# Side pairs of a modulation dealt out anew over two stages of a hybrid diffusion block

## The chip, the cores and the metric

The kernel runs on one core of one Trainium2 chip. The metric is the device time of one execution in microseconds (us), compared as the median of a few timed executions. Beside the timed executions there is one profiled execution, whose rows tell when each instruction ran on the engines: PE (TensorE, matmuls; PEld is its loading of the stationary operand), DVE (VectorE), ACT (ScalarE), POOL (GpSimd) and SP (SyncE, which here only issues transfers).

## The reference, cut to what matters

One layer over 256 latent tokens and 256 context tokens of width 2048, all in 32-bit floats. A vector `c` gives six modulation vectors of 2048 numbers each (`mod`); three of them (`sh1`, `sc1`, `g1`) serve the mixing half, three (`sh2`, `sc2`, `g2`) the MLP half.

```python
mod = (s_lat @ ada_w[l] + ada_b[l])[:, None, :]          # s_lat = silu(c), ada_w: 2048 x 12288
sh1, sc1, g1, sh2, sc2, g2 = jnp.split(mod, N_MOD, axis=-1)
h = modulate(rmsnorm(x, norm1_g[l]), sh1, sc1)
hc = modulate(rmsnorm(xc, norm1_g[l]), csh1, csc1)
q, k, v, f, hy = split_projection(h @ w_in[l])
kc, vc = jnp.split(hc @ w_in[l][:, NA_WIDTH:3 * NA_WIDTH], 2, axis=-1)
a = neighbourhood_attention(heads(q), heads(k), heads(v), kc_h, vc_h, na_rpb[l])
y = merge_groups(a, fourier_mix(f), hyena_mix(hy, ...), mix_norm_g[l])
x = x + g1 * (y @ w_out[l])
x = x + g2 * conv_gated_mlp(modulate(rmsnorm(x, norm2_g[l]), sh2, sc2), *ffn)
return rmsnorm(x, final_norm_g)
```

`sh1` and `sc1` are needed at once and for both token sets. `g1`, `sc2`, `sh2` and `g2` are needed later and for `c` alone: 4 x 2048 numbers, each the dot product of a column of `ada_w` with `silu(c)`. These four vectors are what the change is about.

## The kernel before

**Stages.** The first stage computes k and v for both token sets from the columns 1024 to 3071 of `w_in`. It goes over the 16 slices of 128 rows of the contraction in five blocks of 2, 2, 4, 4 and 4 slices (`blocks`); each block has four groups of output columns (`group`). In the block before, `prep_pieces` computes `sh1` and `sc1` for the next block's rows on PE, from 512 KB loads of `in_ada_t`. The second stage multiplies the rest of `w_in`, in 24 chunks of 512 x 512: chunks 0 to 3 are the Fourier channels, 4 to 15 the three Hyena inputs `u0`, `u1`, `u2`, 16 to 23 the queries. Between the chunks stand the Fourier mix and two long convolutions (`longconv`), each with a forward transform on PE (reads `ftab`), some 13 DVE operations on tiles `X` and `Y`, and a transform back on PE (reads `gtab` and `X`). Then come attention and the output projection, then the MLP.

**A chunk.** Every weight chunk comes as two transfers of 512 KB into tiles named `raw`. ACT rounds each half to `w_hi` (line 173), DVE subtracts to `w_lo` (line 174), and PE makes three matmuls per product (hi-hi, hi-lo, lo-hi), 48 matmuls per chunk in the second stage. There are 8 tiles `raw` and 2 pairs `w_hi`/`w_lo`, so the splitting of chunk k+2 waits until PE has done chunk k.

**Side pairs.** The four late vectors are not computed on PE. For each slice of 128 columns of one vector there are two steps; a step loads 512 KB of `in_ada_col_t` into a `raw` tile of the same ring and DVE multiplies it with `silu(c)` and sums along the row (line 351). Two steps are a pair. `pump(1)` takes a pair from the list `side`; 16 pairs make one vector, and 48 pairs (for `g1`, `sc2`, `sh2`) stand in the list at the start. Where they are taken is set by numbers in `CFG`: `p1` is the number of pairs for each of the five blocks of the first stage, `win` the pairs per chunk in the second stage (fractions are summed up, and a pair is taken for each whole), `att` and `wa` those in attention and projection. What is left then runs before the second norm.

**What sets the order.** The program text gives each piece of work its place, and from it the builder settles one order of instructions for each engine, by when it expects operands to be there; engines run their instructions in that order and wait by semaphores. SP issues nearly all loads in one queue. DVE does, in order, the splits, the side steps, the accumulations of the first stage (line 587), the convolutions (lines 702 and 703) and the long convolutions (lines 184 to 805).

Of the kernel before, what the change touches and what calls it, by code (L numbers as in the profile page):

```python
# [35 lines left out]
for _n, _k in V_LAYOUT:  # L36
# [7 lines left out]

CFG = dict(
    ns=2,
    p1=(0, 0, 2, 6, 9),
    blocks=(2, 2, 4, 4, 4),
    win=(1.5, 0.57),
    att=(1, 0, 1, 4, 0, 1, 0, 0),  # L50
    rest=99,
    start='hp pk x0 x1 h3 dc ft a00 a01 a10 a11 W wm si n1s wp n2s q0 f0 ct c0 c1 e e n0 s0 e e h0 w f1 q1 n1 h1 s1',
    warm=(8, 2),
# [46 lines left out]
def ffn_chunks():  # L100
    out = []
    for kind, g in FFN_PLAN:
        if kind == "up":
            ups = [[("ffn_w_up", k * 4, 4, c, 512) for k in range(4)] for c in (g * 512, DFF + g * 512)]
            out += ups[0] + ups[1] if g else [z for pr in zip(*ups) for z in pr]
        else:
            out += [("ffn_w_down", q * 4, 4, n * 512, 512) for n in range(4) for q in HALVES[g]]
    return out
# [17 lines left out]
def hybrid_block(ctx: ExitStack, tc: tile.TileContext, a: dict, out: bass.AP):  # L126
# [5 lines left out]
    def pool(stack, name, bufs=1, side=None, **kw):  # L132
        return stack.enter_context(tc.tile_pool(name=name, bufs=bufs, side=side, reuse_waits="tile", **kw))
# [173 lines left out]
    w1 = Weights(ctx, 8, 2)  # L307
# [62 lines left out]
    p1 = pool(p1s, "p1", 1, "right")  # L370
# [289 lines left out]
    make_bias()  # L660

    specs = [(a["w_in_t"], i, 4, 512) for i in range(len(WIN_CHUNKS))]
    stream = Stream(w1, specs, 1, lambda j: CFG["win"][j > 5])

    def wide_chunk(stream, ci, pss, hi_src, lo_src, k0, first, last, by_nt=False):
        wh, wl = stream.get(ci)
# [171 lines left out]
    specs = [(a["w_out_t"], i, 4, 512) for i in range(len(WOUT_CHUNKS))]  # L838
    stream = Stream(w1, specs, 1)
# [76 lines left out]
    specs = [(a["ffn_t"], i, 4, 512) for i in range(len(ffn_chunks()))]  # L916
    stream = Stream(w1, specs, CFG["fa"], lambda j: CFG["g2"])
# [180 lines left out]
```

## Time and profile before

| what | us |
|---|---|
| three timed executions | 1297.38, 1318.23, 1319.04 |
| their median | 1318.23 |
| the profiled execution, its own time | 1292.37 |
| span of its rows, first to last instruction | 1290.6 |
| PE busy in the span | 1268.1 |
| DVE busy in the span | 889.5 |
| DMA, mean over the span | 244 GB/s |

The first stage lasts until about 250 us of the span, the second until about 422 us, attention and projection until 558 us, the MLP to the end. A row of the windows view gives for one stretch the busy time and the instruction count of each engine, then the granted clock of PE as a share of full speed, the busy share of the 16 DMA engines, and what they moved in GB/s. Matmuls are pipelined, and one that runs on is counted as busy from its start, so idle time in the PE column is a true wait, while busy time may hide a slower clock.

### The profile page before, as it was taken

To read this page: it belongs to the slowest core of one execution; us is meant where nothing else is said; L and a number is where in the kernel's file an instruction comes from. 1 tells how busy PE (TensorE), PEld (TensorE's weight loads), DVE (VectorE), ACT (ScalarE), POOL (GpSimd) and SP (SyncE) were. 2 spreads that over 40 slices of the span, in tenths; PEclk is the share of its full clock that TensorE was granted. 3 is DMA by queue.
4 is the path that set the end of the run, shared out by engine and by line. 5 is a ranking of instruction groups with operands and counts; after the bars stand their busy time and mean duration, and the time that the engine had idled before them with its cause. 6 is when DMAs were issued, how large, how long until landed. Compare 5 with 4: busy or idle time off the path is not lost.

```text
span 1290.6 us, 24505 instructions
## 1 busy us (share of the span) xinstructions
PE 1268.1 (98%) x10282; PEld 1192.9 (92%) x10282; DVE 889.5 (69%) x1306; ACT 555.5 (43%) x737; POOL 12.0 (1%) x25
## 2 busy tenths in 40 slices
PE   9999999989999999999999999999999999999997
PEld 5768779889899889999999999999999999999997
DVE  5547669968998989987676767744446565655663
ACT  4622212234343665455454545433334444454543
POOL 0000000020000000000000000000000000000000
PEclk9999999999999999999999999999999999999999
DMA  9987878999468855856777777855555656655641
GB/s 365 412 319 288 303 311 306 329 348 323 158 228 325 319 187 173 288 163 222 262 265 257 260 252 263 291 196 196 196 196 183 205 185 199 193 191 191 195 161 66
DMA packets 88399, 315.22 MB, mean 244 GB/s; under 512 B 9952, under 2 KB 10208, under 8 KB 87648
## 3 DMA queue, kind: packets, MB, share of 16 engines
q1 hardware_dynamic: 86944, 311.01, 69.6%
q0 software_dynamic: 768, 1.57, 0.7%
q8 instruction: 80, 1.31, 0.4%
q10 hardware_dynamic: 576, 1.07, 0.2%
q14 instruction: 31, 0.25, 0.1%
HBM read 311.52 MB, written 2.10 MB: 243 GB/s over the span
## 4 chain that ended last, share of the span: by engine, by line
PE 83%; DVE 7%; DMA 6%; ACT 2%; issue 2%; ACTq 0%; DVEq 0%; SPq 0%
PE acc_ps L162 76%; DMA raw<-in_ada_col_t 3%; PE mi_ps L162 3%; DMA raw<-in_w_in_t 3%; PE mi_ps L500 2%; DVE w_lo L174 2%; DVE raw L351 1%; PE mi_ps L170 1%; ACT w_hi L173 1%; DMA pack<-in_pack 0%; DVE Y L788 0%; PE acc_ps L500 0%; DVE bias L658 0%; DVE xr L681 0%; DVE X L795 0%
## 5 line engine op out<-in xcount | busy, mean ns | idle before, releaser
L173 ACT CAST w_hi<-raw 128x1024 fp32r<-128x1024 f32 x376 | 381.3, 1050 | 529.6 <-PE acc_ps L162 444.1
L174 DVE TENSOR_TENSOR w_lo<-raw,w_hi 128x1024 fp32r<-128x1024 f32 x376 | 447.8, 1220 | 221.2 <-ACT w_hi L173 219.9
L162 PE MATMUL acc_ps<-h_hi,w_hi 128*128 128x256 f32 x1408 | 389.0, 277 | 0.5 <-ACT h_hi L256 0.5
L162 PE MATMUL acc_ps<-h_lo,w_hi 128*128 128x256 f32 x1408 | 389.4, 277 | 0.0
L162 PE MATMUL acc_ps<-h_hi,w_lo 128*128 128x256 f32 x1408 | 389.3, 277 | 0.0
L162 PEld LDWEIGHTS acc_ps<-h_hi,w_hi 128*128 128x128 f32 x1408 | 264.2, 188 | 0.6 <-ACT h_hi L256 0.6
L162 PEld LDWEIGHTS acc_ps<-h_hi,w_lo 128*128 128x128 f32 x1408 | 264.5, 188 | 0.0
L162 PEld LDWEIGHTS acc_ps<-h_lo,w_hi 128*128 128x128 f32 x1408 | 264.4, 188 | 0.0
L162 PE MATMUL acc_ps<-yh,w_lo 128*128 128x256 f32 x704 | 194.7, 277 | 0.0
L162 PE MATMUL acc_ps<-yh,w_hi 128*128 128x256 f32 x704 | 194.7, 277 | 0.0
L162 PE MATMUL acc_ps<-yl,w_hi 128*128 128x256 f32 x704 | 194.7, 277 | 0.0
L351 DVE SCALAR_TENSOR_TENSOR raw<-raw,s_row 128x1024 f32<-128x1024 f32 x128 | 154.3, 1218 | 36.4 <-DMA raw<-in_ada_col_t 36.3
L162 PE MATMUL acc_ps<-hx_hi,w_hi 128*128 128x256 f32 x512 | 146.6, 287 | 3.7 <-ACT w_hi L173 3.7
L162 PE MATMUL acc_ps<-hx_hi,w_lo 128*128 128x256 f32 x512 | 143.0, 282 | 1.7 <-DVE w_lo L174 1.7
L162 PE MATMUL acc_ps<-hx_lo,w_hi 128*128 128x256 f32 x512 | 144.0, 282 | 0.0
L162 PEld LDWEIGHTS acc_ps<-yh,w_lo 128*128 128x128 f32 x704 | 132.2, 188 | 0.0
L162 PEld LDWEIGHTS acc_ps<-yh,w_hi 128*128 128x128 f32 x704 | 132.2, 188 | 0.0
L162 PEld LDWEIGHTS acc_ps<-yl,w_hi 128*128 128x128 f32 x704 | 132.2, 188 | 0.0
L162 PEld LDWEIGHTS acc_ps<-hx_hi,w_hi 128*128 128x128 f32 x512 | 97.3, 190 | 9.9 <-ACT w_hi L173 6.8
L162 PEld LDWEIGHTS acc_ps<-hx_lo,w_hi 128*128 128x128 f32 x512 | 97.1, 190 | 2.7 <-issue 2.6
L162 PEld LDWEIGHTS acc_ps<-hx_hi,w_lo 128*128 128x128 f32 x512 | 97.0, 190 | 2.1 <-DVE w_lo L174 2.1
L587 DVE TENSOR_TENSOR kT<-acc_ps,kT 128x512 f32<-128x512 f32 x32 | 22.0, 689 | 28.0 <-PE acc_ps L162 27.9
(245 smaller groups left out, 1530.3 us busy)
## 6 DMA issues: line engine op xcount, KB each, us to landing
raw<-in_ffn_t SPq DMA_DIRECT2D x264, 512.0 KB, 4.3
raw<-in_ada_col_t SPq DMA_DIRECT2D x128, 512.0 KB, 5.2
raw<-in_ada_t SPq DMA_DIRECT2D x64, 512.0 KB, 7.4
raw<-in_w_in_t SPq DMA_DIRECT2D x48, 512.0 KB, 6.5
raw<-in_w_kv_t SPq DMA_DIRECT2D x32, 512.0 KB, 5.8
raw<-in_w_out_t SPq DMA_DIRECT2D x32, 512.0 KB, 4.7
x_in<-in_xT SPq DMA_DIRECT2D x8, 256.0 KB, 5.4
kT<-in_c_tok SPq DMA_DIRECT2D x2, 1024.0 KB, 13.0
```

The costliest lines, as they stand in the source:

```text
L162: return nc.tensor.matmul(ps, lhsT, rhs, start=start, stop=stop, skip_group_check=True)
L170: nc.tensor.transpose(ps, src, ident[:n, :n])
L173: nc.scalar.copy(hi, src)
L174: TT(lo, src, hi.bitcast(F32), op=ALU.subtract)
L351: STT(r, r, 1.0, s_row[:, h * NA : (h + 1) * NA], op0=ALU.mult, op1=ALU.mult, accum_out=sums_[:, f, h : h + 1])
L500: return nc.tensor.matmul(ps[32 * j : 32 * j + 32, :w], s_t[:, kt, :], raws[i // nh][:, kt % nh, :], start=fresh, stop=q == last_q and i i ...
L587: TT(dst, pss[u][:], dst, op=ALU.add)
```

## The change

Two entries of the table and the function that reads one of them:

```diff
-    p1=(0, 0, 2, 6, 9),
+    p1=(0, 0, 4, 6, 7),
-    win=(1.5, 0.57),
+    win=(0.5, 1.0, 0.8),
-    stream = Stream(w1, specs, 1, lambda j: CFG["win"][j > 5])
+    stream = Stream(w1, specs, 1, lambda j: CFG["win"][(j > 3) + (j > 9)])
```

The first stage takes 17 pairs before and after: two of them go from the last block to the third. The second stage takes 19 before (6 x 1.5 + 18 x 0.57 = 19.3) and 19 after (4 x 0.5 + 6 x 1.0 + 14 x 0.8 = 19.2). The sums, loads and matmuls are the same; only places change.

On SP, where the first stage passes into the second, the loads stood like this before (`in_ada_col_t` is a side step, `in_w_in_t` half a chunk; the first row follows the last load of the first stage's weights):

```order
L268 DMA raw<-in_ada_col_t 128x1024 x10
L268 DMA raw<-in_w_in_t 128x1024 x2
L268 DMA raw<-in_ada_col_t 128x1024 x2
L268 DMA raw<-in_w_in_t 128x1024 x2
L268 DMA raw<-in_ada_col_t 128x1024 x4
L732 DMA fc<-in_fou_c 128x128
L733 DMA fl<-in_fou_l 128x2x512
L268 DMA raw<-in_w_in_t 128x1024 x2
```

and now:

```order
L268 DMA raw<-in_ada_col_t 128x1024 x8
L640 DMA gtab<-in_dft_g 128x512
L268 DMA raw<-in_w_in_t 128x1024 x4
L268 DMA raw<-in_ada_col_t 128x1024 x2
L268 DMA raw<-in_w_in_t 128x1024 x4
L732 DMA fc<-in_fou_c 128x128
L733 DMA fl<-in_fou_l 128x2x512
L268 DMA raw<-in_ada_col_t 128x1024 x2
L268 DMA raw<-in_w_in_t 128x1024 x2
```

Ahead of the load of chunk 2 there stand 10 side loads in place of 16, ahead of that of chunk 4 there stand 12 in place of 22, and this difference of 10 stays up to chunk 9.

On DVE, ahead of the second long convolution (whose first own row is L184), the splits of chunks 16 and 17, the side steps and the convolution of `u2` stood like this before:

```order
L351 SCALAR_TENSOR_TENSOR raw,asum<-raw,s_row 128x1024
L353 TENSOR_TENSOR A_70<-asum 128x16
L354 TENSOR_TENSOR A_70<-A_70,pack 128x16
L905 SCALAR_TENSOR_TENSOR A_70<-A_70,pack 128x16
L702 SCALAR_TENSOR_TENSOR u_2823<-acc_ps,pack,u_2823 128x255
L703 SCALAR_TENSOR_TENSOR u_2823<-acc_ps,pack,u_2823 128x255
L174 TENSOR_TENSOR w_lo<-raw,w_hi 128x1024
L702 SCALAR_TENSOR_TENSOR u_2823<-acc_ps,pack,u_2823 128x255 x2
L703 SCALAR_TENSOR_TENSOR u_2823<-acc_ps,pack,u_2823 128x255 x2
L174 TENSOR_TENSOR w_lo<-raw,w_hi 128x1024
L702 SCALAR_TENSOR_TENSOR u_2823<-acc_ps,pack,u_2823 128x255
L184 TENSOR_TENSOR X<-mi_ps,Y 128x512
```

and now:

```order
L351 SCALAR_TENSOR_TENSOR raw,asum<-raw,s_row 128x1024 x2
L702 SCALAR_TENSOR_TENSOR u_2799<-acc_ps,pack,u_2799 128x255
L174 TENSOR_TENSOR w_lo<-raw,w_hi 128x1024
L703 SCALAR_TENSOR_TENSOR u_2799<-acc_ps,pack,u_2799 128x255
L702 SCALAR_TENSOR_TENSOR u_2799<-acc_ps,pack,u_2799 128x255
L351 SCALAR_TENSOR_TENSOR raw,asum<-raw,s_row 128x1024
L702 SCALAR_TENSOR_TENSOR u_2799<-acc_ps,pack,u_2799 128x255
L703 SCALAR_TENSOR_TENSOR u_2799<-acc_ps,pack,u_2799 128x255 x2
L184 TENSOR_TENSOR X<-mi_ps,Y 128x512
```

Two more side steps stand ahead of the long convolution, the three small sums for `sc2` (A_70) have gone behind it, and the split of the second half of chunk 17 (the second L174 of the first list) has gone behind its last row L795.

On PE, the rows just ahead of the transform back of that long convolution were these, where `w_hi_3807` is chunk 18 and `w_lo_3750` chunk 17:

```order
L162 MATMUL acc_ps_3744<-hx_hi_89,w_lo_3750 128x256
L162 MATMUL acc_ps_3743<-hx_hi_89,w_hi_3807 128x256
L162 MATMUL acc_ps_3743<-hx_lo_1394,w_hi_3807 128x256
L162 MATMUL acc_ps_3744<-hx_hi_89,w_hi_3807 128x256
L162 MATMUL acc_ps_3744<-hx_lo_1394,w_hi_3807 128x256
L162 MATMUL mi_ps_3721<-gtab_99,X_3693 128x128
```

and now, where `w_hi_3735` and `w_lo_3736` are chunk 17:

```order
L162 MATMUL acc_ps_3730<-hx_hi_89,w_lo_3736 128x256
L162 MATMUL acc_ps_3729<-hx_hi_89,w_hi_3735 128x256
L162 MATMUL acc_ps_3729<-hx_lo_903,w_hi_3735 128x256
L162 MATMUL acc_ps_3730<-hx_hi_89,w_hi_3735 128x256
L162 MATMUL acc_ps_3730<-hx_lo_903,w_hi_3735 128x256
L162 MATMUL mi_ps_3707<-gtab_99,X_3679 128x128
```

Between the forward transform and the transform back there stood 82 chunk matmuls (30 of chunk 16, 48 of chunk 17, 4 of chunk 18); now there stand 62 (34 of chunk 16, 28 of chunk 17), and the other 20 of chunk 17 come behind the transform back. At the first long convolution there stand 81 now and stood 78.

## The prediction, made before the changed kernel had run

> **What bounds the kernel now.** I read the page first, then a table of windows by stage, then who PE waits for.
>
> ```profile
> span 1290.6 us, 24505 instructions
> PE 1268.1 (98%) x10282; PEld 1192.9 (92%) x10282; DVE 889.5 (69%) x1306; ACT 555.5 (43%) x737; POOL 12.0 (1%) x25
> ...
> L174 DVE TENSOR_TENSOR w_lo<-raw,w_hi 128x1024 fp32r<-128x1024 f32 x376 | 447.8, 1220 | 221.2 <-ACT w_hi L173 219.9
> ...
> L351 DVE SCALAR_TENSOR_TENSOR raw<-raw,s_row 128x1024 f32<-128x1024 f32 x128 | 154.3, 1218 | 36.4 <-DMA raw<-in_ada_col_t 36.3
> ```
>
> PE is busy 98% of the span. Its matmuls are neither added nor removed, so the change can win only PE's idle time and time at a lower clock. A side step costs DVE 1.22 us and half a split 1.22 us. By stage (the stretches are the preparation ahead of the first stage, that stage's third block, its end, then the second stage in three parts, attention, MLP):
>
> ```profile
> core 0: us, PE busy (x) PEld busy (x) DVE busy (x) ACT busy (x) POOL busy (x), PEclk, DMA share, GB/s
> 20.00:40.00 20.00, 18.17 (x125) 10.34 (x124) 16.36 (x39) 9.53 (x16) 0.00 (x0) 1.00 1.03 413
> 94.00:145.00 51.00, 51.00 (x352) 40.59 (x351) 35.42 (x63) 15.05 (x22) 0.00 (x0) 1.00 0.78 283
> 200.00:243.00 43.00, 43.00 (x283) 39.34 (x282) 42.48 (x73) 9.97 (x13) 0.00 (x0) 1.00 0.90 327
> 250.00:312.00 62.00, 56.28 (x454) 54.67 (x453) 47.03 (x73) 24.90 (x32) 10.94 (x17) 1.00 1.01 332
> 312.00:387.00 75.00, 72.83 (x560) 67.61 (x561) 72.09 (x104) 29.59 (x38) 0.00 (x0) 0.98 0.59 205
> 387.00:422.00 35.00, 34.45 (x297) 34.09 (x297) 31.15 (x50) 12.33 (x15) 0.00 (x0) 1.00 0.88 315
> 422.00:558.00 136.00, 133.80 (x992) 121.47 (x991) 120.62 (x227) 78.82 (x141) 0.00 (x0) 1.00 0.70 236
> 558.00:1276.00 718.00, 718.00 (x6333) 717.96 (x6334) 441.13 (x525) 325.36 (x385) 0.00 (x0) 1.00 0.64 210
> ```
>
> The MLP is PE alone: 718.0 of 718 us. The first stage's third block and its end show no idle PE either, though DVE at the end has 42.48 of 43 us. PE idles 62 - 56.28 = 5.7 us in the opening of the second stage, where the DMA engines are full (share 1.01), then 2.2, 0.55 and 2.2 us. In the middle part DMA is slack (0.59) and DVE nearly full (72.1 of 75). So the second stage has two limits one after the other: transfers first, DVE later. What PE waits for in the opening, in two views (the first of 250 to 320 us by PE, the second of 250 to 312 by ACT), and the two large waits in the timeline:
>
> ```profile
> PE acc_ps L162 <- ACT w_hi L173: 3.1, 1, 3.1
> PE mi_ps L170 <- DVE u L703: 1.8, 1, 1.8
> PE acc_ps L162 <- DVE w_lo L174: 0.7, 1, 0.7
> PE mi_ps L162 <- DVE sqf L717: 0.2, 1, 0.2
> ...
> ACT w_hi L173 <- DMA raw<-in_w_in_t: 27.2, 9, 7.0
> ...
> 276.80 0.39 PE L162 MATMUL acc_ps<-hx_hi,w_hi 128*128 128x256 f32 x1 [3.11 <-ACT w_hi L173]
> ...
> 312.13 0.48 PE L170 MATMUL mi_ps<-pack,u 128*128 128x128 f32 x2 [1.78 <-DVE u L703]
> ...
> 310.35 1.23 DVE L351 SCALAR_TENSOR_TENSOR raw<-raw,s_row 128x1024 f32<-128x1024 f32 x1 [1.71 <-DMA raw<-in_ada_col_t]
> ```
>
> PE waits for the rounding of a weight chunk, and ACT waited 27.2 us in nine places for the chunk's transfer. The second large wait has the same root: a side step whose load landed late stood on DVE at 310.35 ahead of the convolution `u` that PE needed. Then comes a cost which the idle column hides:
>
> ```profile
> 313.00:316.40 3.40, 3.40 (x19) 3.40 (x17) 3.40 (x7) 0.56 (x1) 0.00 (x0) 0.52 0.89 325
> ...
> 313.15 0.41 PE L162 MATMUL acc_ps<-hx_hi,w_hi 128*128 128x256 f32 x1
> ...
> 316.35 0.38 PE L162 MATMUL acc_ps<-hx_hi,w_hi 128*128 128x256 f32 x1
> ...
> 557.96 718.56 PE acc_ps L162 x6336
> ```
>
> After the wait at 312 PE ran 3.4 us at 0.52 of its clock. The starts lie 213 ns apart (15 steps in 3.20 us), against 718.56 / 6336 = 113 ns at full clock, so half of 3.4 us is lost: 1.65 us. The opening costs 5.72 + 0.13 (the wait's rest beyond 312) + 1.65 = 7.5 us.
>
> **The change part by part.** *Fewer side loads in the opening.* Ahead of chunk 2's load stand 6 side loads fewer, ahead of chunks 4 to 9 ten fewer. Each is 512 KB; at the 332 GB/s of the opening that is 0.524 MB / 332 = 1.58 us of transfer. Chunk 2 is thus relieved by 9.5 us, chunk 4 onwards by 15.8 us. The waits sum up to some 1 us by chunk 3, about 5 us by the Fourier step and 7.5 us by chunk 9, always less than the relief. Bounds: nothing of the 7.5 us comes back (if bytes are not what fills the engines, below), or all of it. I take all but 0.6 us, for the waits inside the Fourier norm (0.2 for `sqf` in the row above, and its like for the table of ACT), which hang on no transfer: -6.9 us. DVE is relieved of the same ten steps there (12.2 us), so it is not late next; PE is.
>
> [...]
>
> *Two pairs more in the third block, two fewer in the last.* 4 steps x 1.22 = 4.9 us of DVE go where DVE has 51 - 35.4 = 15.6 us idle, and 2.1 MB go where the share is 0.78: at 283 GB/s and that share the engines have room for 0.22 x 51 x 363 GB/s (283 / 0.78) = 4.1 MB. In SP's queue the side loads now also stand ahead of `in_ada_t` loads, and on DVE one stands ahead of the accumulations of line 587 that free the PSUM banks. PE shows no wait in that block; a load that is 1 to 2 us late would be its price, from 0 to 2 us. I take 0, since the same mixture in the fourth and fifth blocks, at 0.90 share, shows PE 43.00 of 43. At the end of the stage DVE gives back 4.9 us of its 42.5.
>
> *Five steps more in chunks 10 to 23.* Counted in DVE's order, the steps between the splits of chunks 1 and 9 fall from 21 to 16, and those up to chunk 23 rise from 17 to 22: 5 x 1.22 = 6.1 us more on DVE, where it has 75 - 72.1 + 35 - 31.15 = 6.8 us idle, though not where one would choose. The place is the second long convolution:
>
> ```profile
> 370.01 3.70 PE L162 MATMUL mi_ps<-zt,ftab 128*128 128x512 f32 x8 [0.42 <-ACT zt L779]
> 383.12 4.30 PE L162 MATMUL mi_ps<-gtab,X 128*128 128x128 f32 x32
> ...
> 371.01 1.21 DVE L174 TENSOR_TENSOR w_lo<-raw,w_hi 128x1024 fp32r<-128x1024 f32 x1
> ...
> 374.84 0.68 DVE L188 TENSOR_TENSOR X<-Y,mi_ps 128x512 f32<-128x512 f32 x1
> ...
> 382.39 2.48 DVE L795 TENSOR_TENSOR X<-Y 128x512 f32<-128x512 f32 x4
> ```
>
> From the end of the forward transform (373.7) to the transform back (383.1) DVE needs 9.4 us, and PE was covered by 82 chunk matmuls x 113 ns = 9.3 us: just enough. Now 62 stand there, 7.0 us, so PE is short by 2.3 us. The cause is the split of chunk 17's second half, which has gone behind the convolution. Besides, two more steps and one split less stand ahead of it on DVE (2.44 - 1.22 - 0.5 for the three small sums), and PE comes 4 matmuls (0.45 us) earlier: DVE is later by 1.2 us against PE, which already waited 0.42 us for `zt` there. Together 3.5 us. Bounds: 0 (if DVE, now unhurried in the opening, comes to that place earlier by as much), or all five steps and the cover, 6.1 + 2.3 = 8.4 us, with a half clock of 1.65 us behind so long a wait. I take 3.5: two split buffers are all the lead DVE can win, and the lead is used up in the first convolution, where the rows are the same as before. The 20 matmuls behind the transform back (2.3 us) then give DVE the lead that it lacked from 387 to 422, so of the 0.55 us idle there I take 0.5 as gone.
>
> *Attention and after.* Totals and rates (`att`, `wa`) stay, one pair is still left over for `rest`. 0, with 2 us either way for an order that the builder has settled anew.
>
> Sum: -6.9 + 3.5 - 0.5 = -3.9 us on the profiled execution: 1292.4 - 3.9 = 1288.5 us. That execution is 5 us below the lowest timed one (1297.38) and 26 us below the median (1318.23), and no row tells why. On the lowest timed run the same sum gives 1293.5; I predict between these, 1290 us.
>
> **The rivals.**
>
> (a) *VectorE takes it back: slower.* The place is chunks 16 to 23, where DVE runs with no lead. If each of the five steps shows on PE, 8.4 + 1.65 = 10.0 us are lost against 6.9 won: +3.1, 1295.5 us on the profiled scale. It decides as soon as more than 6.9 us show. For it speaks DVE's 72.1 of 75 us; against it its 3.9 us idle in 387 to 422 and the 2.3 us of new cover.
>
> (b) *The opening is not relieved: slower by a little, in effect no change.* In the stretch 250 to 312 POOL's 16 bias loads (96 KB in small pieces) run too. The engines move 332 GB/s at share 1.01 there but 413 at 1.03 in the stretch from 20 us. If the small pieces and not the bytes keep them full, fewer side loads help little: the 7.5 us stay and 3.5 - 0.5 come on top, 1295.4 us. [...] Against it: 200 to 243 has no bias loads, and 327 GB/s at 0.90, so most of the loss of rate is there without them; and fewer loads in the queue let the chunk's load start sooner in either case.
>
> (c) *The cover is not missed.* DVE reaches the second convolution early enough: 1292.4 - 6.9 - 0.5 = 1285.0 us.
>
> **How the numbers follow.** Forecast 0.58 (its own range on the profiled scale 1286 to 1291), (a) 0.14, (b) 0.13, (c) 0.15. All of them lie within 0.6% of the profiled time: even PE's whole idle time from 250 to 558 us is 10.6 us, 0.8%. So no case passes 2%, about what a measurement of this kernel can tell from no change, and only the spread of the timed runs themselves (1297 to 1319) can show more: faster 0.07, same 0.89, slower 0.04. The range goes from 1282, with the opening won, nothing lost and 2 us of luck in attention, over 1288.5, (a) and (b) at 1295, to 1315, which is the highest timed run less the forecast's 4 us.
>
> **What would show it.** Right: in 250 to 312 us of the changed kernel PE idles under 1.5 us, ACT's wait for `in_w_in_t` falls from 27.2 us to under 10, and no half clock stands at 313; ahead of the second transform back PE waits 2 to 4 us for `X`, where it waited 0.4. Wrong: a DMA share still at 1.0 with PE idling 5 us in the opening (b); a wait of over 5 us at the second convolution or idle time spread over chunks 18 to 23 (a); new waits of PE in the third block, which I priced at nothing.

## The result and the profile after

The changed kernel takes 1.0069 of the time of the kernel before (95% interval 1.0051 to 1.0087): it is slower by 0.7%, some 9 us, which is little but clear of the noise. Its profiled execution took 1303.74 us, where that of before took 1292.37 and the forecast was 1290. Some executions of every kernel are some 20 to 30 us longer (in the profiles of p1_only, gate_bias, b_gate_bias and b_piece the MLP takes 746.6 us, in that of before 718.6), the ratios leave those executions out, and where a profile below is such a one (the kernels p1_only, gate_bias, b_gate_bias, hold_late, hold3, b_piece, c5) only its rows ahead of the MLP are used.

The windows view of the changed kernel, in the stretches that were shown of before, and the start of the MLP from the chain that ended last:

```profile
core 0: us, PE busy (x) PEld busy (x) DVE busy (x) ACT busy (x) POOL busy (x), PEclk, DMA share, GB/s
94.00:145.00 51.00, 51.00 (x345) 39.16 (x344) 34.72 (x62) 13.86 (x20) 0.00 (x0) 1.00 0.88 308
250.00:312.00 62.00, 54.63 (x423) 53.31 (x422) 40.39 (x62) 21.33 (x28) 11.11 (x18) 0.94 0.99 281
312.00:387.00 75.00, 70.72 (x544) 65.41 (x542) 69.72 (x103) 30.41 (x40) 0.00 (x0) 0.98 0.65 229
387.00:422.00 35.00, 33.12 (x265) 32.82 (x266) 32.95 (x55) 11.03 (x13) 0.00 (x0) 0.90 0.77 276
422.00:558.00 136.00, 133.87 (x995) 121.42 (x994) 120.75 (x219) 77.98 (x136) 0.00 (x0) 1.00 0.73 246
...
569.48 718.55 PE acc_ps L162 x6336
```

The MLP starts 11.5 us later (569.48 against 557.96) and is as long as before (718.55 us against 718.56), so all of the loss lies ahead of it. The opening of the second stage, which was to lose its waits, has more: PE is idle for 62 - 54.63 = 7.4 us, where it was 5.7. The DMA engines are as full as before (0.99) and move less, 281 GB/s in place of 332. The idle time from 312 to 422 grew from 2.7 to 6.2 us.

The waits from 250 to 312 us, all engines; of ACT's wait for `in_w_in_t`, 27.2 us before, nothing is left in this answer:

```profile
DVE raw L351 <- DMA raw<-in_ada_col_t: 15.7, 8, 3.3
ACT sqf L716 <- DVE fo L765: 9.0, 1, 9.0
PE mi_ps L162 <- DVE sqf L717: 6.0, 1, 6.0
PE acc_ps L162 <- DVE w_lo L174: 1.4, 1, 1.4
```

The wait has changed its queue. The weights are early now; it is the side loads that are late (DVE waits 15.7 us for them, 2.0 before), and the steps that need them stand on DVE in order, ahead of the Fourier rows `fo` and `sqf` that PE needs. DVE's part of the timeline there, and the matmul that waited:

```profile
281.99 1.23 DVE L351 SCALAR_TENSOR_TENSOR raw<-raw,s_row 128x1024 f32<-128x1024 f32 x1 [2.21 <-DMA raw<-in_ada_col_t]
...
288.88 1.23 DVE L351 SCALAR_TENSOR_TENSOR raw<-raw,s_row 128x1024 f32<-128x1024 f32 x1 [3.13 <-DMA raw<-in_ada_col_t]
...
290.03 1.28 DVE L765 TENSOR_TENSOR fo<-mi_ps,fq 128x512 f32<-128x512 f32 x2
291.32 1.23 DVE L351 SCALAR_TENSOR_TENSOR raw<-raw,s_row 128x1024 f32<-128x1024 f32 x1
...
292.47 0.69 DVE L717 TENSOR_TENSOR sqf<-sqf 128x512 f32<-128x512 f32 x1
...
293.31 1.84 PE L162 MATMUL mi_ps<-ones,sqf 128*128 128x1 f32 x8 [5.96 <-DVE sqf L717]
```

DVE stands still for 3.13 us at the head of its queue, with `fo` ready behind the step; another step of 1.2 us follows between `fo` and `sqf`. In the kernel before the steps at this place found their data there, and PE waited 0.2 us for `sqf`. The other large wait is the one forecast, at the second long convolution, and at the end of both the clock falls to 0.50. It falls at a third place too, the first long convolution, where a late side load also stands among DVE's rows (the second line below). The fourth clock row lies just ahead of the MLP:

```profile
388.88 6.38 PE L162 MATMUL mi_ps<-gtab,X 128*128 128x128 f32 x32 [4.07 <-DVE X L795]
...
326.11 1.23 DVE L351 SCALAR_TENSOR_TENSOR raw<-raw,s_row 128x1024 f32<-128x1024 f32 x1 [1.57 <-DMA raw<-in_ada_col_t]
...
292.00:298.70 6.70, 5.39 (x25) 5.42 (x26) 4.36 (x9) 3.76 (x5) 1.30 (x2) 0.50 1.07 208
339.70:343.00 3.30, 3.30 (x16) 3.30 (x16) 2.81 (x3) 0.00 (x0) 0.00 (x0) 0.50 0.11 19
387.50:394.20 6.70, 5.33 (x25) 5.36 (x26) 5.56 (x8) 0.00 (x0) 0.00 (x0) 0.50 0.22 45
564.90:568.20 3.30, 3.30 (x18) 3.30 (x17) 1.20 (x6) 0.00 (x0) 0.00 (x0) 0.50 0.00 0
```

Half of the busy time at a clock of 0.50 is lost: 2.7, 1.65, 2.7 and 1.65 us. By idle time and clock the second stage can be laid out. Opening: 7.37 idle + 2.7 = 10.1, against 7.5 before: +2.6. Second long convolution: 4.07 + 2.7 = 6.8. The rest of 312 to 422: idle 4.28 + 1.88 and 1.65 + 2.7 of clock make 10.5, less 6.8 is 3.7, against 2.6 before: +1.1. Together that is 10.5 us. The start of the same matmul in both traces can be set beside it. The second stage begins at 250.69 where it began at 249.84, and attention begins (before, then now) at

```profile
422.41 1.02 PE L162 MATMUL acc_ps<-kT,qT 128*128 128x512 f32 x2
...
432.33 1.02 PE L162 MATMUL acc_ps<-kT,qT 128*128 128x512 f32 x2
```

So the changed kernel is behind by 0.85 us at the end of the first stage, by 9.9 us at the end of the second and by 11.5 us at the MLP: the first stage loses 0.85 us, the second 9.1, attention and projection 1.6, which is about what the clock ahead of the MLP costs. The 10.5 us are thus 1.4 us too high, as an estimate from a column that counts a matmul that runs on as busy; where the 1.4 us lie was not traced.

### The profile page after: what moved, and what is told of

It is laid out like the page before. It is cut to its first block, busy times and chain, and to the rows that moved or that the text cites. A ratio compares the mean times of both kernels' runs of the same rounds, so it can differ in the third digit from the quotient of the medians.

```text
span 1302.0 us, 24500 instructions
## 1 busy us (share of the span) xinstructions
PE 1272.4 (98%) x10282; PEld 1195.3 (92%) x10282; DVE 887.8 (68%) x1306; ACT 555.1 (43%) x737; POOL 12.0 (1%) x25
## 3 DMA queue, kind: packets, MB, share of 16 engines
q0 software_dynamic: 768, 1.57, 1.0%
## 4 chain that ended last, share of the span: by engine, by line
PE 85%; DMA 6%; DVE 6%; issue 1%; ACT 1%; DVEq 0%; SPq 0%; ACTq 0%
PE acc_ps L162 78%; DMA raw<-in_ada_col_t 4%; PE mi_ps L162 3%; PE mi_ps L500 2%; DVE w_lo L174 2%; DMA kT<-in_c_tok 1%; PE mi_ps L170 1%; DVE raw L351 1%; DMA raw<-in_ada_t 1%; ACT w_hi L173 1%; DMA x_in<-in_xT 0%; DVE Y L788 0%; DMA hpack<-in_hpack 0%; DVE bias L658 0%; DVE xr L681 0%
## 5 line engine op out<-in xcount | busy, mean ns | idle before, releaser
L174 DVE TENSOR_TENSOR w_lo<-raw,w_hi 128x1024 fp32r<-128x1024 f32 x376 | 448.0, 1220 | 211.0 <-ACT w_hi L173 209.4
L701 ACT ACTIVATE ga<-acc_ps,pack 128x256 f32<-128x256 f32 x44 | 23.7, 559 | 37.5 <-PE acc_ps L162 31.6
```

The costliest lines, as they stand in the source:

```text
L174: TT(lo, src, hi.bitcast(F32), op=ALU.subtract)
L701: nc.scalar.activation(dst, ps, AF.Identity, bias=b, scale=w1_)
```

## The experiments

There are three theories. A: the place of a side step in VectorE's order, ahead of work that PE needs, is what costs. B: the side loads land late because the 16 bias loads, which run in the opening and come in pieces of 256 bytes, hold the DMA engines. The third: VectorE simply has too much to do.

### Which half of the change carries it

```text
p1_only:   p1=(0, 0, 4, 6, 7), win=(1.5, 0.57) as before
win_only:  p1=(0, 0, 2, 6, 9) as before, win=(0.5, 1.0, 0.8)
```

> Only the first stage's deal is changed (4, 6, 7); the second stage keeps 1.5 and 0.57 per chunk. Theory (the loss is made by the second stage's deal): within 2 us of the kernel before, ratio 0.998 to 1.002, PE idle in the opening of the second stage near 5.7 us as before. Rival (moving two pairs into the third block resettles the order so that it costs by itself): slower by 4 us or more, ratio over 1.003.

> Only the second stage's deal is changed (0.5, 1.0, 0.8); the first stage keeps 2, 6, 9. Theory (the second stage's deal carries the loss): slower than before by 6 to 11 us, ratio 1.005 to 1.0085. Rival (the first stage's deal carries it, or both are needed): within 3 us of before.

Measured: p1_only 1.0027 (1.0006 to 1.0049), win_only 1.0061 (1.0032 to 1.0090). The second stage's deal carries most, as expected; the first stage's deal costs some 3.5 us of its own, which the theory had not. Where p1_only loses it: some 0.9 us in the first stage (the second stage's first matmul starts at 250.76, where it was 249.84), and the most in the opening, where the two waits of the kernel before are there again, a little longer (3.3 and 2.9 us for 3.1 and 1.8), and now both are followed by the half clock, where in before one was:

```profile
PE acc_ps L162 <- ACT w_hi L173: 3.9, 2, 3.3
PE mi_ps L170 <- DVE u L703: 2.9, 1, 2.9
...
278.20:281.40 3.20, 3.20 (x17) 3.20 (x17) 2.50 (x3) 2.27 (x6) 0.65 (x1) 0.50 1.03 360
315.80:319.00 3.20, 3.18 (x15) 3.20 (x16) 3.20 (x6) 1.04 (x2) 0.00 (x0) 0.50 0.87 283
```

### The load or the multiplication

dve_only keeps the multiplications of the 16 side steps of chunks 0 to 9 and drops their loads; load_only does the reverse.

```diff
+                own = 34 <= taken[0] < 50        # dve_only
+                r = w1.raw.tile([P, NA], F32, tag="raw", name="raw")[:] if own else w1.load(...)
+                STT(r, s_row[:, :NA] if own else r, 1.0, s_row[...], ...)
...
+                if 34 <= taken[0] < 50:          # load_only
+                    nc.vector.memset(sums_[:, f, h : h + 1], 0.0)
```

> The changed kernel, but the same 16 side steps multiply a vector that is already in the chip into their tile of the ring, with no load; part of the late modulation vectors is left out. VectorE's work and the ring are as in the changed kernel, 8.4 MB of transfers are gone. Theory (the late landing of a side load blocks VectorE's queue): VectorE never waits there, PE idle in 250 to 312 us under 2.5 us, 6 to 12 us faster than the changed kernel. Rival 1 (bias pieces hold the DMA engines): also relieved, since 16 loads are gone, so this run does not part it from the theory. Rival 2 (VectorE simply has too much to do in the opening and the middle, however soon the loads land): PE idle in the opening stays over 5 us and the total within 3 us of the changed kernel, ratio to before 1.005 to 1.009.

> The changed kernel, but the 16 side steps of the second stage's chunks 0 to 9 keep their load and lose their multiplication on VectorE (a tiny memset of the sum stands in its place), so part of the late modulation vectors is left out; VectorE has 16 x 1.2 = 19.5 us less to do and never stands waiting for these loads, and the transfers are all there. Theory (a late side load blocks VectorE's queue ahead of what PE needs): the 6 us wait of PE near 287 us goes, PE idle in 250 to 312 us falls from 7.4 to under 2.5 us, total 6 to 12 us faster than the changed kernel, level with the kernel before or better (ratio to before 0.997 to 1.002). Rival (the DMA engines are held full by the small pieces of the bias loads): the transfers are the same, so PE idle in the opening stays at 5 us or more and the total stays within 3 us of the changed kernel (ratio to before 1.005 to 1.009).

Measured: dve_only 1.0004 (0.9990 to 1.0019), all of the loss gone with VectorE's work unchanged, so its load is not the cause in the opening (the run does not part A from B, since the late loads themselves are gone). PE still idled 4.9 us there, at another place: the first step that had a load again waited 7.0 us for it and stood ahead of the convolution `u`. load_only went the other way, 1.0152 (1.0128 to 1.0176), which no theory had. Its wait at `sqf` is gone, but the first step that multiplies again waits 20.4 us for its load, and PE behind it:

```profile
PE mi_ps L170 <- DVE u L708: 20.4, 1, 20.4
DVE raw L355 <- DMA raw<-in_ada_col_t: 20.4, 1, 20.4
```

SP, in order, paused between a side load at 304.3 us and the next weight load at 313.9, and the load that VectorE waited for was issued at 318.2. The author's guess, which no run tests, is that SP waited for the ring there, for a tile whose load had not yet landed. The queues in DMA there show what fills the engines meanwhile (300 to 328 us of load_only; q0 is the bias, q1 everything that SP issues; packets, MB, share of 16 engines):

```profile
q1 hardware_dynamic: 1493, 5.42, 53.9%
q0 software_dynamic: 226, 0.44, 27.3%
```

0.44 MB of bias took half as much of the engines as 5.42 MB of large loads. That brought theory B forward.

### The place on VectorE

hold leaves every load where it is and puts eight multiplications behind `sqf`.

```diff
+                if 36 < taken[0] <= 40:
+                    held_steps.append(mult)
+                elif 40 < taken[0] <= 44:
+                    with tc.issue_after(after[0]):
+                        mult()
...
+        with tc.issue_after(last.ins):           # last: the sum for sqf
+            while held_steps:
+                held_steps.pop(0)()
```

> The changed kernel with the same loads in the same queue, but the multiplications of side steps 37 to 44 are held on VectorE until behind the sum of squares of the Fourier norm (sqf); nothing is left out. Theory A (a late side load at the head of VectorE's queue blocks fo and sqf): the 6 us wait of PE near 287 us falls under 1 us and the half clock behind it goes; PE idle in 250 to 312 us falls from 7.4 to under 3.5 us (some 1 to 3 us may come back at dg, behind the six steps now in front of the norm), total 5 to 9 us faster than the changed kernel. Theory B (transfers are the limit, the place on VectorE does not matter): the wait turns into one for the splits of the next weight chunk, since the held tiles keep the ring; PE idle over 5.5 us, total within 3 us of the changed kernel.

Measured: 1.0012 (0.9993 to 1.0032), some 7 us won back. The opening is as theory A said, PE busy in 60.67 of 62 us, its wait for `sqf` 0.18, and the total is within what theory A gave:

```profile
284.27 1.02 PE L162 MATMUL mi_ps<-ones,sqf 128*128 128x1 f32 x8 [0.18 <-DVE sqf L728]
...
250.00:312.00 62.00, 60.67 (x494) 58.56 (x493) 40.77 (x62) 25.19 (x34) 11.11 (x18) 1.00 0.96 266
312.00:387.00 75.00, 66.39 (x485) 61.42 (x484) 72.15 (x105) 26.47 (x35) 0.00 (x0) 0.93 0.63 233
```

But 312 to 387 got worse, 8.6 us idle for 4.3: the held steps shifted the splits, and only 51 chunk matmuls were left to cover the first long convolution (81 in the changed kernel). So the place of the steps is enough to make the opening's wait or to take it away. hold3 went on with it and held steps behind the last rows of both long convolutions too:

```diff
-                if 36 < taken[0] <= 40:
+                if taken[0] in (37, 38, 39, 40, 47, 48, 59, 60):
...
-                elif 40 < taken[0] <= 44:
+                elif taken[0] in (41, 42, 43, 44, 49, 50, 61, 62):
```

> As hold, and besides the multiplications of steps 47 to 50 and 59 to 62 are held until behind the last row that writes X in the first and in the second long convolution; loads and sums as in the changed kernel, nothing left out. The matmuls that cover the two convolutions are then 84 and 83 (51 and 76 in hold, 81 and 62 in the changed kernel). Theory A (every loss is a side step standing ahead of what PE needs on VectorE): no wait for sqf or X over 1.5 us, no half clock behind them; PE idle from 250 to 422 us under 5 us (13.5 in the changed kernel), total 10 to 15 us faster than the changed kernel, ratio to before 0.994 to 0.999. If VectorE has simply too much to do there (72 of 75 us busy from 312 to 387), the steps held back delay the splits instead: PE waits for w_lo of 5 us or more in sum, total as hold within 2 us.

Measured: 1307.1 us, a single time, against a median of 1293.4 for the kernel before: about 1% slower, and no interval. Theory A, as the cause of every loss, fell here. The waits for `X` are gone, and the steps let out behind the convolutions delay the splits instead, as the rival said, by more than it said:

```profile
PE acc_ps L162 <- DVE w_lo L174: 8.5, 2, 4.8
```

### The bias loads, away

late_bias and b_late_bias were meant to issue the bias loads after the first long convolution, by an ordering edge, with the mask moved behind the second.

```diff
-    make_bias()
...
+            with tc.issue_after(back[-1].ins):
+                make_bias()
...
-    hyo='u0 l0 m u1 g0 u2 l1 q0 g1 n q1',
+    hyo='u0 l0 b u1 g0 u2 l1 m q0 g1 n q1',
```

> The changed kernel with the 16 bias loads issued after the first long convolution instead of at the opening of the second stage (and the mask added after the second long convolution); the order of loads on SP and of VectorE up to the first long convolution stays as in the changed kernel. Theory B (the small pieces of the bias loads hold the DMA engines, so side loads land late): the DMA rate in 250 to 312 us rises from 281 to over 330 GB/s, VectorE's waits for in_ada_col_t there fall from 15.7 to under 5 us, PE idle from 7.4 to under 2.5 us; 6 to 10 us faster than the changed kernel, ratio to before 0.998 to 1.003. Theory A (the side loads are placed on VectorE ahead of what PE needs with too little lead, whatever the bias does): PE idle stays over 5 us, the total within 3 us of the changed kernel, ratio to before 1.005 to 1.009.

> The kernel before with the same two moves of the bias loads and of the mask. If the bias pieces also make the waits for the weight chunks in the opening of the kernel before (3.3 us near 273 us and the 1.9 us with the half clock near 312 us): 4 to 7 us faster than before, ratio 0.995 to 0.997, which would beat both kernels. If the bytes and the ring of 8 tiles make them: ratio 0.999 to 1.001.

Measured: 1.0051 (1.0032 to 1.0070) and 1.0043 (1.0024 to 1.0062). Neither tests theory B: the edge, which hangs on a row of VectorE, did not hold POOL's loads, and the profile shows 16 of them in 250 to 312 us as before. They tell what moving the mask does: it costs the kernel before 0.4% (PE idles 5.65 us from 422 to 558 us, where it was 2.2), the changed one nothing (1.0051 with it, 1.0069 without). hold_late adds late_bias to hold:

> Both edits on the changed kernel: bias loads after the first long convolution, and the multiplications of side steps 37 to 44 behind sqf. If A and B are separate causes that add up: 9 to 13 us faster than the changed kernel, ratio to before 0.997 to 1.000, PE idle in 250 to 312 us under 2 us. If they are two handles on one wait: no better than the better of the two alone, within 2 us.

Measured 1.0009 (0.9988 to 1.0031), within hold's interval; it says no more than hold does. gate_bias and b_gate_bias hold the loads back by data:

```diff
         def late_bias():
+            nc.gpsimd.tensor_copy(bias[:, :, 0, 0], z[:, 0, :NH])
+            make_bias()
```

> The changed kernel with the bias loads held back in earnest: a tiny POOL copy of a result of the first long convolution into the bias tile stands ahead of them, so that none runs in 250 to 312 us (in late_bias only the mask moved, the loads did not). VectorE's order up to the first long convolution is as in the changed kernel; at the second one 83 chunk matmuls cover the convolution, where the changed kernel has 62, so some 4 us may be won there by that alone. Theory B (the bias pieces hold the DMA engines, so side loads land late): the rate in the opening rises from 281 to over 330 GB/s, VectorE's waits for in_ada_col_t there fall from 15.7 to under 5 us, PE's 6 us wait at sqf to under 1.5 us; total 8 to 12 us faster than the changed kernel, ratio to before 0.997 to 1.001. Theory A (lead and place on VectorE alone): the wait at sqf stays at 4 us or more; total 2 to 5 us faster, ratio 1.003 to 1.006.

> The kernel before with the same hold on the bias loads (87 matmuls of cover at the second long convolution, 82 before). If the bias pieces make the waits for the weights in its opening (3.3 us near 273 us, 1.9 us and a half clock near 312 us): 4 to 7 us faster than before, ratio 0.995 to 0.997. If bytes and the ring of 8 tiles make them: 0.999 to 1.002.

Measured: 1.0009 (0.9974 to 1.0045) and 1.0034 (1.0002 to 1.0066). The opening of both kernels, first gate_bias, then b_gate_bias:

```profile
250.00:312.00 62.00, 61.92 (x512) 60.73 (x511) 49.12 (x77) 27.32 (x36) 0.57 (x2) 1.00 0.88 304
```

```profile
250.00:312.00 62.00, 61.81 (x507) 60.82 (x506) 52.71 (x83) 27.35 (x36) 0.49 (x2) 1.00 0.91 339
...
PE mi_ps L162 <- ACT Y L181: 9.1, 1, 9.1
```

With no bias load running, neither deal of the side pairs leaves PE idle there. gate_bias came to the total that theory B gave, though two of its signs were missed: 304 GB/s where over 330 was expected, and 5.8 us of waits for side loads where under 5 was. The loads cost at their new place: in b_gate_bias a side load lands 5.2 us late among them, and PE waits 9.1 us in the second long convolution. The expected total of b_gate_bias (4 to 7 us faster) was missed by that.

### The bias loads, in larger pieces

The rows of one head that a partition needs overlap in memory: six rows of 64 numbers, 31 apart, are one run of 5 x 31 + 64 = 219 numbers.

```diff
-                src = bass.AP(..., ap=[[1, GW], [31, 6], [1, GW]])
-                nc.gpsimd.dma_start(half[:, hd], src)
+                src = bass.AP(..., ap=[[1, GW], [1, 219]])
+                nc.gpsimd.dma_start(qT[rp * GW : (rp + 1) * GW, hd, :219], src)
...
+        for m in range(6):
+            TT(bias[:, :, m], qT[:, :, 31 * m : 31 * m + GW], window.unsqueeze(1).to_broadcast([P, NH, GW]), op=ALU.add)
```

> The changed kernel, its bias loaded at the same time and place but in one run of 876 bytes for each partition and head where it had six of 256 bytes (into qT, which is free then); VectorE adds the mask from there in 6 instructions where it had 4. All other rows stand in the same order. Theory B (the small pieces hold the DMA engines, so side loads land late): VectorE's waits for in_ada_col_t in 250 to 312 us fall from 15.7 to under 6 us, PE's 6 us wait at sqf to under 1.5, PE idle there from 7.4 to under 2 us, the half clock behind it goes: 8 to 11 us faster than the changed kernel, ratio to before 0.998 to 1.001 (the 4 us at the second long convolution stay). Theory A (place and lead on VectorE alone): PE idle over 5 us, within 2 us of the changed kernel, ratio 1.005 to 1.009.

> The kernel of a_piece again, for an interval. If the bias's pieces are the cause of all that the changed kernel lost: ratio to before 0.998 to 1.001. If they are part of it: 1.002 to 1.004.

> The kernel before with the same edit. Theory B: its two waits in the opening (3.3 us near 273, 1.9 us and a half clock near 312) go, 5 to 8 us faster than before, ratio 0.994 to 0.996: better than both kernels. If the pieces' form does not matter, 0.999 to 1.001.

> hold (side steps 37 to 44 behind sqf) with the same edit of the bias. If the late landing was the whole cause and the place on VectorE only its path, nothing is left in the opening for it to win: within 2 us of a_piece, or slower by up to 4 us by the shorter cover at the first long convolution (51 matmuls against 81). If the place costs by itself as well: 3 us or more faster than a_piece.

Measured: a_piece gave two times (1293.5 and 1293.8, the kernel before 1293.9 in the median), its repetition a_piece2 0.9996 (0.9979 to 1.0013); b_piece 0.9973 (0.9953 to 0.9994), the one that beats both kernels; hold_piece 0.9998 (0.9970 to 1.0026). An edit that touches neither the side pairs nor the order of any other row (PE's 10282 rows stand in the same order in both traces) brought the changed kernel back to the time of the kernel before. That is not all of what the change costs: with the pieces mended on both sides it is 0.9996 against 0.9973, some 3 us slower, by intervals that overlap. So about two thirds of the 0.69% went with the pieces, and the wait for `X` at the second long convolution is still there (below). The queues in DMA from 250 to 312 us, first of the changed kernel, then of a_piece2:

```profile
q1 hardware_dynamic: 4589, 15.77, 76.2%
q0 software_dynamic: 768, 1.57, 22.0%
```

```profile
q1 hardware_dynamic: 5190, 18.02, 85.0%
q0 software_dynamic: 512, 0.90, 6.2%
```

1.57 MB in 22.0% of 62 us is 115 GB/s while the bias has the engines (180 in the kernel before, where the same loads took 14.1%); the large loads make 334, and the same bias in 876-byte pieces 234. The bias gives back 9.8 us of all engines' time, of which its 0.67 MB fewer bytes explain 2 us at 334 GB/s. The next rows give the median time from a side load's issue to its landing from 250 to 312 us (the last figure, in us), first before, then in the changed kernel, then in a_piece2:

```profile
raw<-in_ada_col_t SPq DMA_DIRECT2D x17, 512.0 KB, 10.8
...
raw<-in_ada_col_t SPq DMA_DIRECT2D x15, 512.0 KB, 8.0
...
raw<-in_ada_col_t SPq DMA_DIRECT2D x16, 512.0 KB, 6.1
```

So the change did not slow a side load down (10.8 before, 8.0 after); it took away the lead with which the load was issued, and with the larger pieces the quicker landing makes up for a part of that. The opening of a_piece2, its waits there, and its wait for `X` from 312 to 422 us:

```profile
250.00:312.00 62.00, 59.52 (x491) 58.14 (x490) 46.72 (x70) 25.47 (x34) 8.79 (x17) 1.00 0.92 307
...
DVE raw L351 <- DMA raw<-in_ada_col_t: 10.7, 4, 4.3
...
PE mi_ps L162 <- DVE X L793: 4.9, 2, 4.0
```

PE idle falls from 7.4 to 2.5 us (under 2 was expected) and no half clock is left there. VectorE still waits 10.7 us for side loads (under 6 was expected), but PE's wait for `sqf` is 0.8 us where it was 6.0. hold_piece is within 2 us of a_piece: late landing and place on VectorE are two ends of one wait, and either mends it. In b_piece the expected 5 to 8 us came to some 3.5: the wait for `u` at 312 went, that for the weights at 272 stayed (2.9 us), and the mean clock of 250 to 312 us is 0.97 there, where it was 1.00 in the kernel before. The size of the pieces does not make this wait. With no bias load there at all (b_gate_bias) it is gone, so the bias loads, or the mask that moved with them, have a part in it; which was not tested.

### The cover at the second long convolution

hold3_gate (hold3 with gate_bias) and two other deals on a_piece:

```diff
-    p1=(0, 0, 4, 6, 7), win=(0.5, 1.0, 0.8)
+    p1=(0, 0, 5, 8, 7), win=(0.5, 1.0, 0.57)     # c1: cover 77 and 82
+    p1=(0, 0, 4, 6, 9), win=(1.5, 1.0, 0.5)      # c5: cover 85 and 83
```

> hold3 with the bias loads held back as in gate_bias (cover 84 and 76). If the bias pieces still cost something once the steps stand right: 1 to 4 us faster than hold3; if not: within 1.5 us of it, or slower where the loads meet the denser transfers after the first long convolution.

> a_piece with three pairs moved from the second stage's later chunks into the first stage: 5, 8, 7 pairs in its last blocks and 0.5, 1.0, 0.57 per chunk; 82 matmuls then cover the second long convolution (62 in a_piece), 77 the first (81). If the short cover makes the wait there: PE's wait of 3.5 us for X near 376 us and the half clock behind it go, 4 to 6 us faster than a_piece, ratio to before 0.994 to 0.997. If VectorE's load makes it, whatever the cover: the wait shrinks by no more than 1.5 us, ratio 0.998 to 1.001. Three pairs more in the first stage cost nothing by the first stage's rows (no idle PE there), up to 4 us if the half clock falls on one of its waits, as in p1_only.

> a_piece with 4, 6, 9 pairs in the first stage's last blocks and 1.5, 1.0, 0.5 per chunk: heavy in the opening, like the kernel before, light behind (cover 85 and 83). If, once the bias's pieces are mended, the opening has room for the side loads: no wait over 2 us there, ratio 0.994 to 0.997, level with b_piece and c1. If the bytes of the side loads limit the opening all the same: waits for the weight chunks of 3 us or more there as in b_piece (2.9 us), ratio 0.997 to 1.000.

Measured: hold3_gate 1.0088 (1.0047 to 1.0129), c1 1.0028 (1.0010 to 1.0046), c5 1.0063 (1.0044 to 1.0083); none is better. In c1, with 82 matmuls of cover PE's waits for `X` from 312 to 422 us are down to

```profile
PE mi_ps L162 <- DVE X L793: 0.3, 1, 0.3
```

where a_piece2 has 4.9. c1 does not show that the cover did it, since it takes three pairs off VectorE as well. hold shows it, at the first long convolution. Here are the transform back of the kernel before, then the forward transform and the transform back of hold:

```profile
334.55 0.71 PE L162 MATMUL mi_ps<-gtab,X 128*128 128x128 f32 x4
...
316.60 3.70 PE L162 MATMUL mi_ps<-zt,ftab 128*128 128x512 f32 x8 [1.16 <-ACT zt L794]
329.99 6.86 PE L162 MATMUL mi_ps<-gtab,X 128*128 128x128 f32 x32 [3.68 <-issue]
```

From the end of the forward transform to the transform back it is 9.7 us in hold (320.30 to 329.99) and 9.7 before (324.90 to 334.55), so VectorE is no later. With 51 chunk matmuls in between (51 x 113 ns = 5.8 us) PE waits 3.7 us, with 78 (8.8 us) it does not wait. (The view names no releaser; the matmul starts as the first row of `X`, begun at 329.21, is done.) In c1, three pairs more in the first stage brought waits there (40.74 us busy of 43 from 200 to 243, where all others had 43.00) and more in the opening. c5 waits 4.7 us for weights in the opening. That is the wait of its second case, but the time is above what either case gave.

## Why the prediction was wrong

**What held.** ACT's wait for the weights fell from 27.2 us to nothing (under 10 was forecast). The half clock at 313 us is gone. PE waits 4.07 us for `X` at the second long convolution: 3.5 were worked out from the 62 matmuls of cover and VectorE's 1.2 us. From the forward transform to the transform back it is 11.1 us now (377.77 to 388.88), less 62 x 113 ns = 7.0 us of cover is 4.1, and hold shows by itself that missing cover makes such a wait. Attention and projection came 1.6 us later, within the 2 us either way that were allowed.

**The step that failed** is the first, "all but 0.6 us" of the opening's 7.5 us credited, and in it the sentence "DVE is relieved of the same ten steps there (12.2 us), so it is not late next; PE is". VectorE's work was the wrong thing to look at (dve_only: same work, no loss). What counts is when its loads land; the prediction had such a case in its own row at 310.35, and took it to go with the number of loads. With 1.5 pairs per chunk from the start the side loads ran ahead and the weights were late; with half a pair the weights are ahead and the side loads late. The DMA engines are full in both (1.01 and 0.99), and a late side load stops VectorE's whole queue (3.13 us ahead of the step at 288.88), `fo` and `sqf` included. In place of -6.9 stands +2.6.

**The rival that came nearest** is (b), the small pieces of the bias loads, given 0.13. The row it rests on (332 GB/s at share 1.01 against 413 at 1.03) was read rightly. The counter-argument, that 200 to 243 us moves 327 GB/s without bias, was weaker than it looked, for there the engines were not full (0.90): per full engines it is 401, 363 and 329 GB/s, so about half of the loss of rate was there without the bias, not most. a_piece2 and the two gated kernels show that the pieces hold the loads back (a side load lands in 6.1 us in a_piece2, in 8.0 in the changed kernel); but (b) took the waits to stay as they were, 1295.4 us, and they grew. How they grew, through the order on VectorE, was in no rival. It takes both: better pieces mend the opening with the steps in place (a_piece2), and moved steps mend it with the pieces as they were (hold).

**A term of the wrong size.** The second long convolution cost 6.8 us, not 3.5: the wait was right, and the half clock behind it (2.7 us) had been priced only in rival (a). With the opening's it makes 5.4 us that the sum lacked.

**Small terms.** The 0.5 us from 387 to 422 came: all of the 1.88 us idle there is the end of the wait for `X`, and behind it, from 389 to 422, PE is busy throughout. The two pairs moved in the first stage were bounded by 0 and 2 us and taken as 0; the stage lost 0.85 us, though its third block shows no idle PE (345 matmuls ran in those 51 us where it was 352). p1_only costs 0.27%, 0.06 to 0.49, the most of it further on, in the opening. At the end of the stage DVE did not get its 4.9 us back from 200 to 243: it is busy for 43.00 of 43 us there. From the forecast -3.9 to the measured +11.4 us of the profiled executions it is 15.3: the second stage 13.0 (+9.1 for -3.9, and in it, by idle time and clock, the opening 9.5 and the long convolution 3.3), attention and projection 1.6, the first stage 0.85.

**What stays open.** Why the same bias loads took 14.1% of the engines in the opening before and 22.0% after was not tried. The first stage's 0.85 us and the half clock ahead of the MLP were not tried either, nor was what is left of the change's cost once the pieces are mended.

## What to carry to other kernels

Where DMA engines are full, look first at who fills them for how few bytes: the queue table's share against its MB finds it in one line (27.3% for 0.44 MB beside 53.9% for 5.42 MB in load_only), and part of the remedy may have nothing to do with the transfers that are being dealt out. Work that waits for a load and is not urgent did harm here in an in-order queue ahead of work that was (VectorE stood 3.13 us with `fo` ready, PE 5.96 us for `sqf`): the loads were dealt out "by need", to arrive just in time, and here that was late. Moving that work behind is no remedy by itself: hold gained some 7 us by it, and hold3, with more steps moved, lost them again and more in late splits. Ask also what covers a long wait: the 20 matmuls that left their place (2.3 us) made more of the 4.1 us than VectorE's being later (1.7 us). Four waits of PE of some 3 us were followed up: three came with a slower clock that made them nearly 5 (2.9 and 3.3 us in p1_only, 2.9 in b_piece), one did not (3.1 us in before); the waits of 4.07 and 5.96 us in the changed kernel cost 2.7 us more than themselves by it.

## What the runs showed of the hardware

The clock. Here is what the clock was at PE's waits. After a wait of 3.1 us (before, 273.7) it stayed at 1.00 (276.8 to 312); after one of 1.8 us (before) it was 0.52 from 313.0 to 316.4, and after those of 3.3 and 2.9 us (p1_only) it was 0.50 in the 3.2 us shown of each. At the waits of 5.96 and 4.07 us (after) it was 0.50 for some 6.8 us, from some 1.4 us ahead of the wait's end on; at one of 3.68 us (hold) it was 0.50 from 329.5 to 336.1. For the wait of 4.0 us in a_piece2 there is only the mean of 312 to 387 us, 0.98, from which some 3 us at 0.50 can be estimated. The stretches of the changed kernel begin at 291.9, 339.6, 387.4 and 564.9 us and last some 6.8, 3.4, 6.8 and 3.4 us. Ahead of the second stand waits of 0.57 and 0.89 us (up to 336.87 and 338.49), and ahead of the fourth PE idles 0.14 us in all from 552 to 564.9. So in these traces the length of the last wait does not tell by itself whether the clock falls, nor for how long; what does was not shown.

Small pieces. In the changed kernel the bias moved 115 GB/s of engine time in pieces of 256 bytes, where the large loads made 334; in a_piece2 it moved 234 in pieces of 876 bytes, still short of the large loads there (18.02 MB in 85.0% of 62 us, 342 GB/s). The same pieces of 256 bytes made 180 in the kernel before, so their size alone does not set the rate.
